# A decoder layer's second down projection in scaled float16 pairs, with sums of w_down and seven PSUM banks in turn

## The chip, the cores and the metric

The kernel runs on one core of a Trainium2 chip. The metric is the device time of one execution in microseconds (us), as a median over several runs. The core's engines are TensorE (PE in the profile; its weight loads are PEld), VectorE (DVE), ScalarE (ACT), GpSimd (POOL) and SyncE (SP, whose queue issues nearly all DMA transfers here). Each engine takes its instructions in the order in which the program gives them, and engines wait for each other through semaphores.

## The reference

The layer takes x of 2048 rows by 1024 columns and one condition vector. In order: a normalised and modulated x goes through one combined projection; eight heads of forgetting attention and a gated short convolution share its columns; their outputs go through `w_out` and are added to x. The second block is the one that matters here:

```python
h2 = rmsnorm(x, norm2_g) * (1 + sc2) + sh2
u = causal_dwconv(h2 @ w_up, ffn_conv_w)      # 1024 -> 2 x 2816, three taps over the rows
u_gate, u_val = jnp.split(u, 2, axis=-1)
y = (jax.nn.silu(u_gate) * u_val) @ w_down    # 2816 -> 1024, the down projection
return x + g2 * y
```

All inputs and the output are float32. `g2` is a row of 1024 gates that comes from the condition vector.

## The kernel before, in words

Every float32 product is made of three TensorE products of two parts, high and low: high x high, high x low, low x high (helper `mm3`, line 142). The parts are either float32r tiles or float16 tiles. Float16 parts need their operands scaled into float16's range, so stages that use them first find the largest magnitude of both operands, take powers of two from it, multiply by these when they split, and divide the result again. Float32r parts need no scale.

The feed-forward block goes in two halves of 1024 rows, `for hv in range(2)`: first the up projection `up(hv)`, then the down projection `down(hv, side)`.

`up(hv)` goes over 22 column blocks of 128 (`NPAIR = 22`). A block is seven products of 12 float16 matmuls (line 1253); VectorE and ScalarE combine them, apply three taps, silu and the gate product, and write y for the block to `y_sc` in DRAM. The last steps of a block, `finish`, run while TensorE is in the next block, and those of the last block run in the down projection that follows, as the first part of `side`. At the end of the 22 blocks `first_pairs(hv)` loads three pairs for the down projection and splits them.

`down(hv, side)` goes over four groups n (two blocks of 512 rows by two blocks of 512 output columns) of 22 steps i each. A step uses one pair: a `raw` tile whose first 512 columns are y of block i, transposed, and whose last 512 are the rows of `w_down` of block i. `load_pair` fills it (lines 1218 and 1219) and `split_pair` makes the float32r parts: ScalarE copies to `hi` (line 1224), VectorE subtracts to `lo` (line 1225). Four PSUM tiles `acc` of 128 rows by 512 columns take the products, 3 matmuls each, 12 per step. Steps 20 and 21 of a group run together, tile after tile, so that the four tiles end one after the other. Then `add_gated` (lines 1070 and 1071) multiplies each by the gates, adds x and stores the rows. `hi`, `lo` and `raw` have four buffers each. In the program a pair is split two steps before its use and loaded five steps before. `acc` comes from `ps_d`, which has four of the eight PSUM banks; `ps_u` has three more, which the up projection uses in its odd blocks, and `ps_n` one.

In the first half, `side` also has the second half's preparation, a piece at each even step: row norms of eight 128-row tiles (`norm2(2)` and `norm2(3)`: squares at line 1111, a root in small VectorE steps, a scaling at line 1118), then per column block four transposes on TensorE into the one bank of `ps_n` (line 1094), a read-out (line 1096) and float16 parts (lines 1077 and 1080). After these come the first weights of the second up projection.

The order of the work is the order of the code: nearly all instructions are pinned by `keep_in_program_order`, separately for each engine. A semaphore wait stands where a tile is read after a write, or written after a read, by another engine.

Of the kernel before, what the change touches and what calls it, by code (L numbers as in the profile page):

```python
# [20 lines left out]
P = 128  # L21
S = 2048
D = 1024
# [7 lines left out]
NPAIR = DFF // P  # L31
# [8 lines left out]
HS = 1.0  # L40
LINES = 528
NTEMP = 7


@with_exitstack
def kernel(
# [20 lines left out]
    V, A, G, T = nc.vector, nc.scalar, nc.gpsimd, nc.tensor  # L67
    x, c, out = x[0], c[0:1], out[0]
# [69 lines left out]
    K = tc.keep_in_program_order  # L138
# [597 lines left out]
    def load_out(n):  # L736
# [9 lines left out]
            lambda: K(A.activation(wo["junk"][:, 0:512], t, AF.Abs, accum_out=sums[:, n : n + 1])),  # L746
        )

    def out_scales(pool):
# [8 lines left out]
        K(V.tensor_reduce(gm[:, 0:1], pt[0:2, 0:P], axis=AX.X, op=ALU.max))  # L758
        K(V.tensor_scalar(gm, ident[0:2, 0:2], gm[:, 0:1], None, op0=ALU.mult))
# [3 lines left out]
        bits = osc.bitcast(I32)  # L763
        K(V.tensor_scalar(osc, pt[:, 0:2], 2.0**-40, 2.0**60, op0=ALU.max, op1=ALU.min))
        K(V.tensor_scalar(bits, bits, 0x7F800000, None, op0=ALU.bitwise_and))
        K(V.reciprocal(osc, osc))
        K(V.tensor_scalar(bits, bits, 0x7F800000, None, op0=ALU.bitwise_and))
        K(V.tensor_scalar(osc, osc, 16384.0, None, op0=ALU.mult))
        K(V.tensor_tensor(oinv, osc[:, 0:1], osc[:, 1:2], op=ALU.mult))
        K(V.reciprocal(oinv, oinv))  # L770
        yield

    def load_mixed(Q, i):
# [282 lines left out]
    with ExitStack() as ph:  # L1056
# [7 lines left out]
        def wide_temp():  # L1064
            return fp.tile([P, 1040], F32, tag="w4", name="w4", bufs=5)[:, 0:1026]

        def add_gated(acc, gate, src, dst):

            g = temp()
            K(V.tensor_tensor(g, acc, gate, op=ALU.mult))  # L1070
            K(V.tensor_tensor(src, src, g, op=ALU.add))
            nc.sync.dma_start(dst, src)

        bt = {}

        def high(raw, hi):
            K(A.activation(hi, raw, AF.Copy))  # L1077
# [21 lines left out]
        def norm2(Q):  # L1099

            if Q == 0:
                fp.tile([P, 96], F32, name="rim2")
            ss = fp.tile([P, 16], F32, tag="ss", name="ss", bufs=2)[:, 0:4]
            xn[Q] = kept[Q] if Q < 2 else [wide_temp()[:, 0:D] for _ in range(4)]
            if Q >= 2:
                for t in range(4):
                    K(nc.sync.dma_start(xn[Q][t], x1_sc[Q * 4 + t]))
                yield
            for t in range(4):
                junk = fp.tile([P, D], BF16, tag="t2", name="junk", bufs=NTEMP)  # L1110
                K(A.activation(junk, xn[Q][t], AF.Square, accum_out=ss[:, t : t + 1]))
                if t % 2:
                    yield
            K(V.tensor_scalar(ss, ss, 1.0 / D, EPS, op0=ALU.mult, op1=ALU.add))
            for ins in rsqrt_steps(fp, ss, 4, "r"):
                K(ins)
            for t in range(4):
                K(V.tensor_scalar(xn[Q][t], xn[Q][t], ss[:, t : t + 1], None, op0=ALU.mult))
# [36 lines left out]
            if Q % 2:  # L1155
                low(t4, *t4s)
                yield
# [56 lines left out]
        def load_pair(n, i):  # L1214

            Q, hf = divmod(n, 2)
            raw = raw_tile()
            K(nc.sync.dma_start(raw[:, 0:512], y_sc[i][:, Q * 512 : (Q + 1) * 512]))
            K(nc.sync.dma_start(raw[:, 512:1024], w_down[i * P : (i + 1) * P, hf * 512 : (hf + 1) * 512]))
            return raw  # L1220

        def split_pair(raw):
            hi, lo = pair_tiles()
            K(A.activation(hi, raw, AF.Copy))  # L1224
            K(V.tensor_tensor(lo, raw, hi.bitcast(F32), op=ALU.subtract))  # L1225
            y, wd = halves((hi, lo))
            return (*y, *wd)

        raws, pairs = {}, {}

        def first_pairs(hv):

            for i in range(3):
                raws[4 * hv, i] = load_pair(4 * hv, i)
            yield
            for i in range(3):
                pairs[4 * hv, i] = split_pair(raws.pop((4 * hv, i)))
                yield
            while True:
                yield  # L1240

        def up(hv):
# [25 lines left out]
            def finish(i, p1, Y, gate, val, yg):  # L1268

                taps(yg, gate, i)  # L1270
                add(val[:, 2:514], p1, Y)
                yield
                yv = tap(val, NPAIR + i)
                keep_halo(val, NPAIR + i)
                K(A.activation(yg, yg, AF.Silu))
                taps(yv, val, NPAIR + i)
                yield
                K(V.tensor_tensor(yv, yg, yv, op=ALU.mult))
                nc.sync.dma_start(y_sc[i][:, hv * 1024 : (hv + 1) * 1024], yv)
                yield  # L1280

            wts, ops = ready.pop("wts"), ready.pop("ops")
            last = None
            for i in range(NPAIR):
                o11, o12, os2, os4, os3, o22, os1 = ops
                X, Y, Z = [
# [37 lines left out]
                yg = tap(gate, i)  # L1324
                keep_halo(gate, i)
                next(wts)
                product(Y, o22, "t4", False)
                last = finish(i, p1, Y, gate, val, yg)
            return last

        def down(hv, side):

            todo = [(n, i) for n in range(4 * hv, 4 * hv + 4) for i in range(NPAIR)]
            loaded = split = 3
            for e, (n, i) in enumerate(todo):
                Q, n0 = n // 2, n % 2 * 512
                rows = [slice((Q * 4 + t) * P, (Q * 4 + t + 1) * P) for t in range(4)]
                while split < min(e + 3, len(todo)):
                    if loaded == split:
                        raws[todo[loaded]] = load_pair(*todo[loaded])  # L1340
                        loaded += 1
                    pairs[todo[split]] = split_pair(raws.pop(todo[split]))
                    split += 1
                while loaded < min(e + 6, len(todo)):
                    raws[todo[loaded]] = load_pair(*todo[loaded])
                    loaded += 1
                if i == 0:
                    acc = [ps_d.tile([P, 512], F32, tag="d", name="acc") for _ in range(4)]
                if i == NPAIR - 3:
                    xs = [fb.tile([P, 512], F32, tag=f"src{n % 2 * 4 + t}", name="xs") for t in range(4)]  # L1350
                    for xp, r in zip(xs, rows):
# [8 lines left out]
                    next(side, None)  # L1360
                if i == NPAIR - 1:
                    for t in range(4):
                        add_gated(acc[t], gates[:, D + n0 : D + n0 + 512], xs[t], out[rows[t], n0 : n0 + 512])
            for _ in side:
                pass

# [39 lines left out]
```

## Time and profile before

| what | us |
|---|---|
| median of 3 runs (lowest, highest) | 2449.33 (2448.84, 2451.18) |
| the profiled execution's own time | 2450.66 |
| its span from first to last instruction | 2448.8 |
| TensorE busy | 2366.2 |
| first half's down projection, start to end | 1554 to 1806 |
| second half's up projection | 1806 to 2204 |
| second half's down projection | 2204 to the end |

The stage borders come from the chain of waits, where TensorE's groups of matmuls change their line (1253 in the up projection, 142 in the down projection). Matmuls are pipelined and their ends are modelled, so the length of one is not what it costs; in a run without breaks its cost is the time from one start to the next. In a row of a timeline the columns are start, length, engine, line, operation, output and inputs, count, and in brackets the idle time before it with what ended it. In a row of the groups the two numbers behind the bar are the busy time of all and the mean of one in ns. A wait is given to the semaphore that came last.

### The profile page before, as it was taken

The numbers are of one execution on the slowest core, as the hardware profiler recorded it, in microseconds if no ns is written. First come the engines' busy times: TensorE is split into PE (matmuls) and PEld (weight loads), VectorE is DVE, ScalarE is ACT, GpSimd is POOL, SyncE is SP. The second block draws the span as 40 slices with busy tenths as digits, with TensorE's granted clock in tenths as the row PEclk, the third lists the DMA queues.
The fourth block names the chain that finished last, engine by engine and source line by source line (L and its number), as shares of the span: only waits on it lengthen the run. The fifth ranks groups of instructions, "written<-read, shape, count | busy, mean of one in ns | idle before, by whom it ended". The sixth has DMA issues, their size and how long they took to land.

```text
span 2448.8 us, 38397 instructions
## 1 busy us (share of the span) xinstructions
PE 2366.2 (97%) x14451; PEld 1590.2 (65%) x14451; DVE 1773.1 (72%) x3329; ACT 1262.6 (52%) x2024; POOL 336.4 (14%) x282
## 2 busy tenths in 40 slices
PE   5999999999898888999999999999999999999999
PEld 5988788888676666444444444688864444448887
DVE  6567884542798888556888888757768888885554
ACT  5433453220688887343666565555545556554333
POOL 0210101101567785001000000000000000000000
PEclk9999999999999999999999999999999999999999
DMA  9344686543699988534222222677742222236775
GB/s 278 116 131 125 179 239 184 159 134 90 123 187 166 213 166 159 184 104 155 78 86 86 87 88 76 202 241 225 226 146 81 91 86 86 87 100 215 228 228 184
DMA packets 428706, 368.70 MB, mean 151 GB/s; under 512 B 184208, under 2 KB 327912, under 8 KB 427496
## 3 DMA queue, kind: packets, MB, share of 16 engines
q1 hardware_dynamic: 421400, 349.40, 51.1%
q10 hardware_dynamic: 4752, 8.46, 1.0%
q0 software_dynamic: 2368, 8.39, 0.9%
q8 instruction: 113, 1.85, 0.3%
q14 instruction: 73, 0.60, 0.1%
HBM read 267.54 MB, written 65.08 MB: 136 GB/s over the span
## 4 chain that ended last, share of the span: by engine, by line
PE 79%; DVE 7%; issue 5%; DMA 4%; ACT 3%; POOL 1%; SPq 0%; ACTq 0%; DVEq 0%; POOLq 0%
PE acc L1253 33%; PE acc L142 25%; PE pr L142 11%; PE pv L142 3%; DMA far<-wide 2%; PE pt L937 1%; PE ps L876 1%; DMA wx<-in_w_up_dram 1%; PE ps L877 1%; DVE near L944 1%; DVE s_t L900 1%; PE po L973 1%; ACT s_t L917 1%; PE po L975 1%; PE po L974 1%
## 5 line engine op out<-in xcount | busy, mean ns | idle before, releaser
L1253 PEld LDWEIGHTS <-pair 128*128 128x128 f16 x3696 | 361.4, 98 | 436.2 <-issue 0.3
L1253 PE MATMUL acc<-t,pair 128*128 128x512 f16 x2112 | 477.4, 379 | 0.0
L1253 PE MATMUL acc<-b,pair 128*128 128x512 f16 x1584 | 363.5, 379 | 0.0
L1225 DVE TENSOR_TENSOR lo<-raw,hi 128x1024 fp32r<-128x1024 f32 x176 | 211.9, 1223 | 153.6 <-ACT hi L1224 153.3
L142 PE MATMUL acc<-hi 128*128 128x512 f32 x704 | 276.8, 393 | 1.6 <-DVE t L1070 1.6
L142 PE MATMUL acc<-lo,hi 128*128 128x512 f32 x704 | 274.3, 390 | 0.5 <-DVE lo L1225 0.5
L142 PE MATMUL acc<-hi,lo 128*128 128x512 f32 x704 | 274.3, 390 | 0.0
L1224 ACT ACTIVATE hi<-raw 128x1024 fp32r<-128x1024 f32 x176 | 182.4, 1055 | 178.2 <-PE acc L142 141.2
L1266 DVE SCALAR_TENSOR_TENSOR w<-w,fcw,w 128x1024 f32<-128x1024 f32 x176 | 226.1, 1285 | 34.7 <-ACT w L1261 25.4
L1077 ACT ACTIVATE pair<-raw 128x1024 f16<-128x1024 f32 x132 | 138.3, 1048 | 68.4 <-DVE raw L1160 68.3
L142 PE MATMUL acc<-wp,mp 128*128 128x512 f16 x768 | 171.1, 382 | 1.0 <-DVE raw L829 1.0
L1261 ACT ACTIVATE w<-w,fcw 128x1024 f32<-128x1024 f32 x88 | 100.7, 1144 | 130.7 <-DVE w L1159 130.7
L917 ACT ACTIVATE s_t<-s_t,nb,cst 128x2048 f32<-128x2048 f32 (+15 forms) x128 | 164.7, 1288 | 4.8
L1080 DVE TENSOR_TENSOR pair<-raw,pair 128x1024 f16<-128x1024 f32 x132 | 160.7, 1218 | 4.7 <-ACT pair L1077 4.7
L608 ACT ACTIVATE wx<-wx 128x512 f32<-128x512 f32 x88 | 55.6, 632 | 198.8 <-DMA wx<-in_w_up_dram 171.1
L142 PE MATMUL pr<-hh,wh 128*128 128x512 f32 x384 | 153.4, 399 | 0.0
L142 PEld LDWEIGHTS acc<-hi 128*128 128x128 f32 x704 | 132.2, 188 | 31.2 <-DVE t L1070 4.4
L142 PE MATMUL pr<-hl,wh 128*128 128x512 f32 x384 | 151.1, 393 | 0.0
L142 PE MATMUL pr<-hh,wl 128*128 128x512 f32 x384 | 150.8, 393 | 0.2 <-DVE wl L179 0.2
L142 PEld LDWEIGHTS acc<-lo,hi 128*128 128x128 f32 x704 | 132.3, 188 | 27.8 <-DVE lo L1225 1.0
L142 PEld LDWEIGHTS acc<-hi,lo 128*128 128x128 f32 x704 | 132.2, 188 | 27.7
L929 POOL TENSOR_TENSOR wide<-s_t,wide 128x1024 f16<-128x1024 f32 x64 | 136.9, 2138 | 5.3
(296 smaller groups left out, 4694.4 us busy)
## 6 DMA issues: line engine op xcount, KB each, us to landing
raw<-in_w_up_dram SPq DMA_DIRECT2D x88, 512.0 KB, 3.9
raw<-y_sc SPq DMA_DIRECT2D x176, 256.0 KB, 4.3
raw<-in_w_down_dram SPq DMA_DIRECT2D x176, 256.0 KB, 6.1
wx<-in_w_up_dram SPq DMA_DIRECT2D x88, 256.0 KB, 3.1
y_sc<-w SPq DMA_DIRECT2D x44, 512.0 KB, 2.6
wm<-in_w_ada_dram SPq DMA_DIRECT2D x128, 128.0 KB, 2.8
wr<-in_w_in_dram SPq DMA_DIRECT2D x40, 256.0 KB, 3.9
x_t<-in_x_dram SPq DMA_DIRECT2D x16, 512.0 KB, 5.5
```

Source lines behind the costliest of these rows:

```text
L142: ins = T.matmul(acc, lhsT=a, rhs=b, start=st, stop=sp)
L608: K(A.activation(t, t, AF.Abs, accum_out=l1[:, n : n + 1]))
L876: K(T.matmul(ps[:, 0:cw], lhsT=qt, rhs=kh[:, c0 : c0 + cw], start=True, stop=False))
L917: K(A.activation(cols, cols, AF.Exp, bias=nb[:, p : p + 1], scale=qk[:, 4:5], accum_out=un["l"][:, p : p + 1]))
L929: K(G.tensor_tensor(wide[:, 1, :], s_t[:, WB * P : WU], wide[:, 0, :], op=ALU.subtract))
L1077: K(A.activation(hi, raw, AF.Copy))
L1080: K(V.tensor_tensor(lo, raw, hi, op=ALU.subtract))
L1224: K(A.activation(hi, raw, AF.Copy))
L1225: K(V.tensor_tensor(lo, raw, hi.bitcast(F32), op=ALU.subtract))
L1253: K(T.matmul(acc, lhsT=a, rhs=b, start=st, stop=sp, skip_group_check=True))
L1261: K(A.activation(y, u[:, 0:1024], AF.Copy, scale=fcw[:, ct : ct + 1]))
L1266: K(V.scalar_tensor_tensor(y, u[:, m : m + 1024], fcw[:, m * 44 + ct : m * 44 + ct + 1], y, op0=ALU.mult, op1=ALU.add))
```

## The change

In the second half, `split_pair` makes float16 pairs for the first 20 of the 22 blocks (`LAST = 20`): one instruction per engine for y and one for `w_down`, each with its power of two. Blocks 20 and 21 keep float32r parts, scaled alike. `add_gated` multiplies by the inverse scale too. The scales come from sums of absolute values, per partition, an upper bound for the largest magnitude. For `w_down` they are taken in the first half's groups n = 0 and 1: after each split, ScalarE writes the absolute values of the pair's `w_down` half over itself and keeps the sum. For y they are taken in the second up projection, one ScalarE instruction of 128x1024 per block for blocks 0 to 19. In its last block, `first_pairs(1)` reduces both, with two small TensorE products, and the vector helper `powers_of_two` (moved out of `out_scales` unchanged) makes the scales. In both halves `first_pairs` now splits two pairs, later in the last block, and the third is split at the start of `down`. The PSUM tiles of the groups take the banks of `ps_d` and `ps_u` in turn, seven in all.

The core of the diff:

```diff
-        def split_pair(raw):
-            hi, lo = pair_tiles()
-            K(A.activation(hi, raw, AF.Copy))
-            K(V.tensor_tensor(lo, raw, hi.bitcast(F32), op=ALU.subtract))
-            y, wd = halves((hi, lo))
-            return (*y, *wd)
+        def split_pair(n, e, i, raw):
+
+            if n < 4:
+                hi, lo = pair_tiles()
+                K(A.activation(hi, raw, AF.Copy))
+                K(V.tensor_tensor(lo, raw, hi.bitcast(F32), op=ALU.subtract))
+                if n < 2:
+                    K(A.activation(raw[:, 512:1024], raw[:, 512:1024], AF.Abs, accum_out=big["rim"][:, 52 + n * NPAIR + i : 53 + n * NPAIR + i]))
+                y, wd = halves((hi, lo))
+                return (*y, *wd)
+            scales = big["rim"][:, 46:48]
+            if i < LAST:
+                t = fq.tile([P, 2048], F16, tag=("hi", "lo")[e % 2], name="yw", bufs=4)
+                parts = [[t[:, (2 * n + m) * 512 : (2 * n + m + 1) * 512] for m in range(2)] for n in range(2)]
+            else:
+                parts = halves(pair_tiles())
+            for n, (hi, lo) in enumerate(parts):
+                half, sc = raw[:, n * 512 : (n + 1) * 512], scales[:, n : n + 1]
+                K(A.activation(hi, half, AF.Copy, scale=sc))
+                K(V.scalar_tensor_tensor(lo, half, sc, hi if i < LAST else hi.bitcast(F32), op0=ALU.mult, op1=ALU.subtract))
+            return (*parts[0], *parts[1])
...
         def first_pairs(hv):
 
+            rim = big["rim"]
+            om, sc, inv, gm = rim[:, 44:46], rim[:, 46:48], rim[:, 48:49], rim[0:2, 50:52]
             for i in range(3):
                 raws[4 * hv, i] = load_pair(4 * hv, i)
-            yield
-            for i in range(3):
-                pairs[4 * hv, i] = split_pair(raws.pop((4 * hv, i)))
+            if hv:
+                K(V.tensor_reduce(om[:, 0:1], rim[:, 0:LAST], axis=AX.X, op=ALU.max))
+                K(V.tensor_reduce(om[:, 1:2], rim[:, 52 : 52 + 2 * NPAIR], axis=AX.X, op=ALU.max))
+            yield
+            if hv:
+                pt = ps_n.tile([P, 512], F32, tag="n", name="pt")
+                K(T.transpose(pt[0:2, 0:P], om, ident))
+                K(V.tensor_reduce(gm[:, 0:1], pt[0:2, 0:P], axis=AX.X, op=ALU.max))
+                K(V.tensor_scalar(gm, ident[0:2, 0:2], gm[:, 0:1], None, op0=ALU.mult))
+            yield
+            if hv:
+                pt = ps_n.tile([P, 512], F32, tag="n", name="pt")
+                K(T.matmul(pt[:, 0:2], lhsT=ones[0:2, :], rhs=gm, start=True, stop=True))
+                powers_of_two(pt[:, 0:2], sc, inv)
+            yield
+            yield
+            for i in range(2):
+                pairs[4 * hv, i] = split_pair(4 * hv, i, i, raws.pop((4 * hv, i)))
                 yield
...
+                if hv and i < LAST:
+                    junk = fp.tile([P, D], BF16, tag="t2", name="junk", bufs=NTEMP)
+                    mags.append(lambda: K(A.activation(junk, yv, AF.Abs, accum_out=big["rim"][:, i : i + 1])))
                 nc.sync.dma_start(y_sc[i][:, hv * 1024 : (hv + 1) * 1024], yv)
...
-            loaded = split = 3
+            loaded, split = 3, 2
...
-                    acc = [ps_d.tile([P, 512], F32, tag="d", name="acc") for _ in range(4)]
+                    acc = []
+                    for c in range(4 * (n - 4 * hv), 4 * (n - 4 * hv) + 4):
+                        acc.append((ps_d if c % 7 < 4 else ps_u).tile([P, 512], F32, tag="d" if c % 7 < 4 else "u", name="acc"))
```

The gating becomes `scalar_tensor_tensor(g, acc, inv, gate, mult, mult)` in the second half.

What moves on ScalarE's queue, in the first half's down projection, group n = 0, around the first column of the second half's preparation. `hi` is a pair's high half, `t2` the read-out of four transposes, `b11` and `b21` its float16 high part. Before:

```order
L1224 ACTIVATE hi_18297<-raw_18242 128x1024 [waits DMAHW0_49,DMAHW7_49,DVE_49,PE_49]
L1096 ACTIVATE t2_18321<-pt_18316,sh2_137,a2_136 128x512 [waits PE_49]
L1077 ACTIVATE b11_18323<-t2_18321 128x512 [waits Activation_49]
L1224 ACTIVATE hi_18326<-raw_18261 128x1024 [waits DMAHW2_49,DMAHW1_49,DVE_49]
L1224 ACTIVATE hi_18345<-raw_18282 128x1024 [waits DMAHW4_49,DMAHW3_49,DVE_49]
L1096 ACTIVATE t2_18369<-pt_18364,sh2_137,a2_136 128x512 [waits PE_49]
```

With the change, at the same place (L1237 is the absolute sum of `w_down`, L1234 the high half, L1104 the read-out, L1085 the high part):

```order
L1234 ACTIVATE hi_18313<-raw_18256 128x1024 [waits DMAHW7_49,DMAHW0_49,PE_49]
L1237 ACTIVATE raw_18256,rim2_13816<-raw_18256 128x512 [waits DVE_49]
L1104 ACTIVATE t2_18338<-pt_18333,sh2_137,a2_136 128x512 [waits PE_49]
L1085 ACTIVATE b11_18340<-t2_18338 128x512 [waits Activation_49]
L1234 ACTIVATE hi_18343<-raw_18276 128x1024 [waits DMAHW2_49,DMAHW1_49]
L1237 ACTIVATE raw_18276,rim2_13816<-raw_18276 128x512 [waits DVE_49]
L1234 ACTIVATE hi_18363<-raw_18298 128x1024 [waits DMAHW4_49,DMAHW3_49]
L1237 ACTIVATE raw_18298,rim2_13816<-raw_18298 128x512 [waits DVE_49]
L1104 ACTIVATE t2_18388<-pt_18383,sh2_137,a2_136 128x512 [waits PE_49]
```

Behind each high half stands a sum that waits for VectorE and writes the `raw` tile that the low half reads.

On TensorE's queue, in the last block of the second up projection, between its second product (operand `t2`) and its third (operand `b21`). Before:

```order
L1253 LDWEIGHTS pair_22914
L1253 MATMUL acc_23030<-t2_19634,pair_22914 128x512
L1253 LDWEIGHTS pair_22915
L1253 MATMUL acc_23030<-t2_19634,pair_22915 128x512
L1253 LDWEIGHTS pair_22912
L1253 MATMUL acc_23029<-b21_18371,pair_22912 128x512 [waits Activation_49]
```

With the change:

```order
L1293 LDWEIGHTS pair_22996
L1293 MATMUL acc_23114<-t2_19678,pair_22996 128x512
L1293 LDWEIGHTS pair_22997
L1293 MATMUL acc_23114<-t2_19678,pair_22997 128x512
L1266 MATMUL pt_23169<-ident_117,rim2_13816 2x128 [waits DVE_49,PE_49]
L1293 LDWEIGHTS pair_22994
L1293 MATMUL acc_23113<-b21_18390,pair_22994 128x512 [waits Activation_49]
```

The small transposition of the two maxima stands between the products and waits for VectorE. The second small product, of the same kind, stands one product later.

More of the change, by code (lines that the diff above doesn't have):

```diff
@@ L42 @@
 NTEMP = 7
+LAST = 20
 @with_exitstack
@@ L747, in load_out, with powers_of_two @@
         )
+    def powers_of_two(src, s, inv):
+        bits = s.bitcast(I32)
+        K(V.tensor_scalar(s, src, 2.0**-40, 2.0**60, op0=ALU.max, op1=ALU.min))
+        K(V.tensor_scalar(bits, bits, 0x7F800000, None, op0=ALU.bitwise_and))
+        K(V.reciprocal(s, s))
+        K(V.tensor_scalar(bits, bits, 0x7F800000, None, op0=ALU.bitwise_and))
+        K(V.tensor_scalar(s, s, 16384.0, None, op0=ALU.mult))
+        K(V.tensor_tensor(inv, s[:, 0:1], s[:, 1:2], op=ALU.mult))
+        K(V.reciprocal(inv, inv))
     def out_scales(pool):
@@ L1065, in wide_temp, with add_gated @@
             return fp.tile([P, 1040], F32, tag="w4", name="w4", bufs=5)[:, 0:1026]
-        def add_gated(acc, gate, src, dst):
+        def add_gated(hv, acc, gate, src, dst):
             g = temp()
-            K(V.tensor_tensor(g, acc, gate, op=ALU.mult))
+            if hv:
+                K(V.scalar_tensor_tensor(g, acc, big["rim"][:, 48:49], gate, op0=ALU.mult, op1=ALU.mult))
+            else:
+                K(V.tensor_tensor(g, acc, gate, op=ALU.mult))
             K(V.tensor_tensor(src, src, g, op=ALU.add))
             nc.sync.dma_start(dst, src)
-        bt = {}
+        bt, big = {}, {}
         def high(raw, hi):
@@ L1101, in norm2 @@
             if Q == 0:
-                fp.tile([P, 96], F32, name="rim2")
+                big["rim"] = fp.tile([P, 96], F32, name="rim2")
             ss = fp.tile([P, 16], F32, tag="ss", name="ss", bufs=2)[:, 0:4]
@@ L1283, in up @@
             last = None
+            mags = []
             for i in range(NPAIR):
@@ L1341, in down @@
                         loaded += 1
-                    pairs[todo[split]] = split_pair(raws.pop(todo[split]))
+                    pairs[todo[split]] = split_pair(todo[split][0], split, todo[split][1], raws.pop(todo[split]))
                     split += 1
@@ L1362, in down @@
                     for t in range(4):
-                        add_gated(acc[t], gates[:, D + n0 : D + n0 + 512], xs[t], out[rows[t], n0 : n0 + 512])
+                        add_gated(hv, acc[t], gates[:, D + n0 : D + n0 + 512], xs[t], out[rows[t], n0 : n0 + 512])
             for _ in side:
```

13 lines of the change are left out of this document (5 added, 8 removed).

## The prediction

> **What bounds the kernel now.** I read the page first, then the chain of waits from 1400 us on, then the busy times by stage. Times in all fences are microseconds from the span's start unless marked ns. From the page:
>
> ```profile
> span 2448.8 us, 38397 instructions
> PE 2366.2 (97%) x14451; PEld 1590.2 (65%) x14451; DVE 1773.1 (72%) x3329; ACT 1262.6 (52%) x2024; POOL 336.4 (14%) x282
> ```
>
> TensorE carries the program, so two things can move the time: how far apart matmuls start, and moments in which TensorE waits for split operands. The chain of waits shows the first (start, length, what):
>
> ```profile
> 1805.90 398.88 PE acc L1253 x1848
> 2204.78 235.32 PE acc L142 x1038
> ```
>
> The up projection (float16) starts a matmul every 398.88 / 1848 = 215.8 ns, the second half's down projection (float32r) every 235.32 / 1038 = 226.7 ns. Both run without a break. The busy times by stretch show the first column group of the first half's down projection, then the second up projection:
>
> ```profile
> core 0: us, PE busy (x) PEld busy (x) DVE busy (x) ACT busy (x) POOL busy (x), PEclk, DMA share, GB/s
> 1554.40:1619.00 64.60, 64.20 (x290) 52.43 (x288) 42.71 (x55) 33.44 (x41) 0.00 (x0) 1.00 0.72 236
> 1806.00:2204.40 398.40, 398.40 (x1848) 180.52 (x1847) 347.73 (x389) 227.84 (x302) 0.00 (x0) 1.00 0.28 88
> ```
>
> TensorE is all but full at the whole clock, ScalarE is half idle. By these shares 0.6 us more ScalarE work per pair would be free. But a pair is made in a chain over two engines, and the change lengthens that chain.
>
> **The change part by part.** *The sums of w_down (the main term).* In the first half's groups n = 0 and 1, each of 44 splits gets a third step: ScalarE writes the high half, VectorE subtracts the low half, and then ScalarE takes absolute values in place over the half of `raw` that VectorE has just read. So this step waits for the low half (the order shows a wait on VectorE at L1237), and ScalarE's next instruction, the next pair's high half, stands behind it. High, low and sum of one pair follow the sum of the pair before: a loop. Its lengths, from timelines of ScalarE and VectorE and from the groups:
>
> ```profile
> 2300.04 1.06 ACT L1224 ACTIVATE hi<-raw 128x1024 fp32r<-128x1024 f32 x1 [1.66 <-PE acc L142]
> 2301.13 1.23 DVE L1225 TENSOR_TENSOR lo<-raw,hi 128x1024 fp32r<-128x1024 f32 x1 [1.49 <-ACT hi L1224]
> ...
> L746 ACT ACTIVATE junk<-wo 128x512 bf16<-128x512 f32 x16 | 9.9, 622 | 0.0
> ...
> 1729.48 0.61 DVE t L1087
> ...
> 1730.12 0.77 ACT t L1077 x2
> ```
>
> High to low 1.09 us (2300.04 to 2301.13), low half 1.23, VectorE to ScalarE 0.03 (the chain piece at 1730), the sum 0.62 as in L746, the nearest row, also absolute values of 128x512 with a sum: 2.97 us. TensorE uses up a pair in 12 x 226.7 = 2.72 us. From here ScalarE sets the pace, and whatever else it or VectorE does in between adds in full:
>
> ```profile
> 1553.80 1.04 ACT L1224 ACTIVATE hi<-raw 128x1024 fp32r<-128x1024 f32 x1
> 1557.08 1.16 ACT L1261 ACTIVATE w<-w,fcw 128x1024 f32<-128x1024 f32 x1 [2.23 <-DVE w L1159]
> ...
> 1601.67 0.78 ACT L1096 ACTIVATE t<-pt,sh,a 128x512 f32<-128x512 f32 x1 [2.59 <-PE pt L1094]
> ...
> 1603.02 2.00 ACT L1224 ACTIVATE hi<-raw 128x1024 fp32r<-128x1024 f32 x2
> ...
> 1654.00 1.04 ACT L1111 ACTIVATE junk<-w 128x1024 bf16<-128x1024 f32 x1
> ...
> 1655.04 1.04 ACT L1111 ACTIVATE junk<-w 128x1024 bf16<-128x1024 f32 x1
> ...
> 1584.03 0.16 DVE L1114 TENSOR_SCALAR ss<-ss 128x4 f32<-128x4 f32 x1
> 1586.40 1.42 DVE L1118 TENSOR_SCALAR w<-w,ss 128x1024 f32<-128x1024 f32 x2
> ...
> 1558.26 2.60 DVE L1266 SCALAR_TENSOR_TENSOR w<-w,fcw,w 128x1024 f32<-128x1024 f32 x2
> 1614.41 0.68 DVE L1070 TENSOR_TENSOR t<-acc,gates 128x512 f32<-128x512 f32 x1
> 1619.71 1.22 DVE L1225 TENSOR_TENSOR lo<-raw,hi 128x1024 fp32r<-128x1024 f32 x1
> ```
>
> - 8 normalised columns, each a read-out and a high half between two splits, 1601.67 to 1603.02 = 1.35: 10.8. One more read-out alone: 0.7.
> - 8 squares of 1.04 (1654.00 to 1655.04): 8.3.
> - 2 row-norm scalings on VectorE, 1584.03 to 1587.82 = 3.8. VectorE idles 2.97 - 1.23 = 1.74 per loop, so 2.05 of each shows: 4.1.
> - Gating group n = 0, 1614.41 to 1619.71 = 5.3 on VectorE, less the same 1.74: 3.5.
> - The last up column's rest (tap 1.16 and silu of the same size on ScalarE; on VectorE four taps, 1.3 each): 2.6 where ScalarE has to wait for both, 1.3 where only VectorE is late: 3.9.
>
> Sum of these: 31.3 us. Pair 1's high half starts at about 1553.8, as the first one behind the tap does today. Pair 43's then starts at 1553.8 + 42 x 2.97 + 31.3 = 1709.8; its low half is done 2.3 later, at 1712.1, and 24 matmuls (5.4) end group 1 at 1717.5. Today:
>
> ```profile
> 1680.67 0.48 PE L142 MATMUL acc<-hi 128*128 128x512 f32 x1
> 1681.98 0.50 PE L142 MATMUL acc<-hi 128*128 128x512 f32 x1 [0.36 <-DVE t L1070]
> ```
>
> Group 2 begins at 1680.67, so TensorE is 37 us late. From there no sums are taken, and I add 1 for the refill of the pairs behind the next gating: **+38**. Bounds: with a loop of 2.72 instead of 2.97, +27; with 0.1 more per pair for hand-overs, and raw buffers late by as much again, +45. I take the row values.
>
> *Seven banks.* Today TensorE waits for gating at the three group ends of the first half: the fence above shows two matmuls of one tile's start 1.31 apart instead of 0.68. All such waits together are small:
>
> ```profile
> PE acc L142 <- DVE t L1070: 1.6, 5, 0.4
> ```
>
> In starts lost that is about 3 us. With three free banks they go, but at the first two ends pairs are late anyway, which the 38 already has; at most 0.8 at the third end is kept, and it lies inside that rounding. Second half: no waits, nothing to gain.
>
> *Float16 in the second half.* 4 groups x 20 pairs x 12 = 960 matmuls change type: 960 x (226.7 - 215.8) = **-10.4**. A switch from float16 to float32r costs once:
>
> ```profile
> 2204.43 0.58 PE L142 MATMUL acc<-hi 128*128 128x512 f32 x1
> 2204.84 0.39 PE L142 MATMUL acc<-lo,hi 128*128 128x512 f32 x1
> 2205.07 0.39 PE L142 MATMUL acc<-hi,lo 128*128 128x512 f32 x1
> ```
>
> 0.41 instead of 0.23. The last two pairs of each group stay float32r: three switches more, **+0.6**. The splits become two instructions on each engine:
>
> ```profile
> L781 ACT ACTIVATE mp<-src,rim 128x512 f16<-128x512 f32 x32 | 22.1, 712 | 11.7 <-DVE wp L782 11.7
> L782 DVE SCALAR_TENSOR_TENSOR mp<-src,rim,mp 128x512 f16<-128x512 f32 x32 | 23.4, 749 | 11.9 <-ACT mp L781 11.8
> ```
>
> 1.42 and 1.50 per pair in a step of 12 x 215.8 = 2.59: hidden by TensorE. Not so at the start: only two pairs are split ahead instead of three, and VectorE has four low halves (6.0) and five column instructions (5.9) from about 2205 on before pair 4, wanted 4 x 2.59 = 10.4 after TensorE's start at 2204.4. That is late by 1.7 (0 to 3): **+1.7**.
>
> The Trainium skill, page "TensorE: Matmul & The Clock Gate", section "Back-to-back issue gap", gives a warm matmul N/2.4 + 2.5 ns, 215.8 at 512 columns, whatever its type. The float16 rows agree, the float32r rows lie 10.9 above. By the rule alone the type would bring nothing.
>
> *The scale.* Two tiny matmuls enter TensorE's queue in the last up column, the second behind VectorE's maximum and scaling; today VectorE does that pair of operations, for w_out, in
>
> ```profile
> L759 DVE TENSOR_SCALAR rim<-ident,rim 2x2 f32<-2x2 f32 x1 | 0.7, 731 | 0.0
> L758 DVE TENSOR_REDUCE rim<-pt 2x1 f32<-2x128 f32 x1 | 0.3, 280 | 0.1
> ```
>
> Here they follow an addition that today begins at 2193.46 and takes 0.68, so they end near 2195.1. TensorE arrives at 2194.25, after the third product of the column:
>
> ```profile
> 2193.46 0.68 DVE L1159 TENSOR_TENSOR t<-t,acc 128x512 f32<-128x512 f32 x1
> 2194.25 5.34 PE L1253 MATMUL acc<-t,pair 128*128 128x512 f16 x24
> ```
>
> 0.8 of waiting, two type switches and two small matmuls: **+1.5** (0.5 to 3).
>
> *The rest.* 20 sums over y in the second up projection, some 1.04 each: ScalarE is busy 227.84 of 398.4 there and 21 more fit; the next queued read-out waits for TensorE anyway. 0, or up to 21 if that cover went. The final gating multiplies twice, 746 ns (L829 is this form on a PSUM tile) for 685, four times behind the last matmul: **+0.2**.
>
> ```profile
> L829 DVE SCALAR_TENSOR_TENSOR raw<-acc,rim,raw 128x512 f32<-128x512 f32 x16 | 11.6, 746 | 13.3 <-PE acc L142 13.2
> L1070 DVE TENSOR_TENSOR t<-acc,gates 128x512 f32<-128x512 f32 x32 | 21.9, 685 | 9.0 <-PE acc L142 9.0
> ```
>
> Sum: 38 - 10.4 + 0.6 + 1.7 + 1.5 + 0.2 = +31.6 on the profiled execution's 2450.7 (its span 2448.8 and 1.9 around it): 2482.3. It lies 1.3 above the median of the runs, so 2481.0.
>
> **The rivals.** *The sums are free* (faster). If ScalarE's sum found the low half done, because VectorE kept far enough ahead, or the next high half did not queue behind it, 38 would become -0.8 or so: 2481 - 39 = 2442. It decides as soon as the loop, with all that stands in it, is under TensorE's pace, 2.72. For it: the half-idle ScalarE, and buffers for four pairs. Against it: two high halves run back to back (1603.02, x2) right after the read-out of a column, so waiting instructions do hold those behind them; and 2.97 is over 2.72 before anything else is added.
>
> *A shorter loop* (slower, less). With 2.72 per loop the +27 gives 2470; should half of the listed extras also overlap, 16 less, about 2455.
>
> *Loads join the loop* (slower still). A `raw` buffer is now free after the sum instead of after the low half. From the page's DMA issues:
>
> ```profile
> raw<-in_w_down_dram SPq DMA_DIRECT2D x176, 256.0 KB, 6.1
> ```
>
> Landing takes 6.1 us. With four buffers a load has three loops, 8.9, for issue and landing. At 10.3 for both, each loop is (10.3 + 2.97) / 4 = 3.3: 42 x 0.35 = 15 more, 2496. TensorE's slower pace thins the traffic, which speaks against it.
>
> *Float16 brings nothing.* Without the -10.4: 2491. Against it stand w_out's products, float16 pairs through the same helper, 382 ns a matmul where float32r has 390:
>
> ```profile
> L142 PE MATMUL acc<-wp,mp 128*128 128x512 f16 x768 | 171.1, 382 | 1.0 <-DVE raw L829 1.0
> L142 PE MATMUL acc<-hi,lo 128*128 128x512 f32 x704 | 274.3, 390 | 0.0
> ```
>
>
> **How the numbers follow.** What this kernel's measurement can tell from no change is about 0.2%, 5 us. Forecast 72%, 2481, its own range 2468 to 2488 from the bounds +27 and +45. Shorter loop 9%, of which 2 within 0.2% of today; loads 7%; no gain from float16 4%; free sums 8%, of which 1 ends within 0.2%. Faster 7%, same 3%, slower 90%. The range for 8 in 10 is 2465 to 2490: it leaves out the free sums, the shortest loop and most of the loads.
>
> **What would show it.** In the changed kernel's first down projection, groups 0 and 1 should last about 82 us each instead of 64, TensorE idle before `acc` until the low half, ScalarE's sums idle 1.2 to 1.3 us each before them until `lo`, and the sum group x44 at about 0.62. Groups 2 and 3 should keep 61 to 64. The second down projection should start matmuls 216 ns apart, 227 in the last 24 of each group, with a break of 1 to 2 us near pair 4. If ScalarE's sums show no wait for `lo`, the main term is wrong; if the up projection gets breaks, the y sums are not hidden.

## The result and the profile after

The change makes the kernel slower. The median is 2478.1 us (2474.09 to 2479.35, 4 runs) against 2450.26 us (2448.84 to 2454.34, 4 runs) for the kernel before. The ratio is 1.0113, with a 95% interval of 1.0098 to 1.0128. The profiled execution took 2478.72 us, with a span of 2477.0. Forecast were 2481 us and a range of 2465 to 2490.

The head of the page of the kernel after:

```profile
span 2477.0 us, 38721 instructions
PE 2371.2 (96%) x14454; PEld 1506.9 (61%) x14454; DVE 1793.0 (72%) x3428; ACT 1333.3 (54%) x2240; POOL 336.3 (14%) x282
```

The shares hardly move (ScalarE from 52% to 54%, TensorE from 97% to 96%), and from them alone nobody would find 28 us. The stages do show it. The table gives the time from a stage's first matmul to the next stage's first one, from TensorE's timeline; the last column is the time from the last matmul's start to the end of the span.

| kernel | start of the 1st up projection | 1st up | 1st down | 2nd up | 2nd down | tail |
|---|---|---|---|---|---|---|
| before | 1155.40 | 398.67 | 251.67 | 398.68 | 239.35 | 5.06 |
| after | 1154.51 | 398.67 | 289.33 | 399.58 | 229.71 | 5.21 |
| difference | -0.89 | 0 | +37.66 | +0.90 | -9.64 | +0.15 |

The part ahead of the first up projection holds nothing of the change and differs between executions: it starts there between 1149.9 and 1155.8 in the eleven profiles of this case. What follows repeats to some hundredths of a microsecond wherever two kernels have the same code. So the experiments below are read by these stages, and by the medians for the whole.

The first down projection loses 37.66 us, and the second gains 9.64. The busy times by stretch of the kernel after show its first three column groups and the second up projection:

```profile
core 0: us, PE busy (x) PEld busy (x) DVE busy (x) ACT busy (x) POOL busy (x), PEclk, DMA share, GB/s
1553.20:1635.60 82.40, 71.63 (x282) 53.14 (x281) 42.12 (x51) 48.92 (x86) 0.00 (x0) 0.94 0.62 190
1635.60:1714.90 79.30, 71.21 (x289) 53.17 (x288) 39.66 (x53) 47.65 (x84) 0.00 (x0) 0.96 0.60 191
1714.90:1782.00 67.10, 64.73 (x286) 52.45 (x285) 52.83 (x65) 32.92 (x42) 0.00 (x0) 0.97 0.65 209
1842.50:2242.10 399.60, 399.49 (x1853) 181.13 (x1853) 347.28 (x399) 244.98 (x341) 0.00 (x0) 1.00 0.27 86
```

In the same columns, groups n = 0 and 1 of the kernel before:

```profile
1554.07:1615.87 61.80, 61.80 (x281) 51.12 (x280) 39.98 (x51) 32.93 (x41) 0.00 (x0) 1.00 0.72 235
1615.87:1679.77 63.90, 63.38 (x290) 51.76 (x288) 39.99 (x54) 33.80 (x42) 0.00 (x0) 1.00 0.76 251
```

Groups n = 0 and 1, where sums of `w_down` are taken, last 82.4 and 79.3 us; before, they lasted 61.8 and 63.9. ScalarE is idle for 33.5 of the 82.4, so it isn't short of time. What it waits for stands in its timeline:

```profile
1571.57 1.04 ACT L1234 ACTIVATE hi<-raw 128x1024 fp32r<-128x1024 f32 x1
1573.90 0.63 ACT L1237 ACTIVATE raw<-raw 128x512 f32<-128x512 f32 x1 [1.29 <-DVE lo L1235]
1574.44 0.19 ACT L1237 ACTIVATION_READ_ACCUMULATOR raw<-raw 128x1 f32 x1
1574.53 1.05 ACT L1234 ACTIVATE hi<-raw 128x1024 fp32r<-128x1024 f32 x1
```

and in VectorE's, in the same microseconds:

```profile
1572.64 1.22 DVE L1235 TENSOR_TENSOR lo<-raw,hi 128x1024 fp32r<-128x1024 f32 x1 [1.74 <-ACT hi L1234]
```

From 1571.57 to 1574.53 one turn takes 2.96 us: high half on ScalarE, low half on VectorE, sum on ScalarE, next high half. ScalarE idles 1.29 per turn for VectorE, VectorE 1.74 for ScalarE, and TensorE wants a pair every 2.72. In the waits ScalarE's row for this has one entry for each of the 44 sums (first fence, ScalarE, first half's down projection), and nearly all of TensorE's own waits are for the two parts of a pair (second fence, from there to the end):

```profile
ACT raw L1237 <- DVE lo L1235: 68.3, 44, 4.8
...
ACT hi L1234 <- DMA raw<-y_sc: 3.0, 1, 3.0
...
ACT hi L1234 <- DMA raw<-in_w_down_dram: 1.0, 1, 1.0
```

```profile
PE acc L143 <- DVE lo L1235: 15.2, 18, 1.9
PE acc L143 <- ACT hi L1234: 4.4, 6, 1.0
```

### The profile page after: what moved, and what is told of

Same layout as the page of the kernel before. It is cut to its first block, busy times and chain, and to the rows that moved or that the text cites. A ratio compares the mean times of both kernels' runs of the same rounds, so it can differ in the third digit from the quotient of the medians.

```text
span 2477.0 us, 38721 instructions
## 1 busy us (share of the span) xinstructions
PE 2371.2 (96%) x14454; PEld 1506.9 (61%) x14454; DVE 1793.0 (72%) x3428; ACT 1333.3 (54%) x2240; POOL 336.3 (14%) x282
## 4 chain that ended last, share of the span: by engine, by line
PE 73%; DVE 9%; issue 6%; DMA 6%; ACT 5%; POOL 2%; SPq 0%; ACTq 0%; DVEq 0%; POOLq 0%
PE acc L1293 32%; PE acc L143 20%; PE pr L143 11%; PE pv L143 3%; DVE lo L1235 2%; DMA wx<-in_w_up_dram 2%; DMA far<-wide 2%; PE pt L942 1%; ACT hi L1234 1%; DVE near L949 1%; PE ps L881 1%; DVE s_t L905 1%; PE ps L882 1%; PE po L978 1%; DMA raw<-in_w_down_dram 1%
## 5 line engine op out<-in xcount | busy, mean ns | idle before, releaser
L143 PE MATMUL acc<-yw 128*128 128x512 f16 x960 | 208.0, 379 | 0.6 <-DVE yw L1249 0.6
L1085 ACT ACTIVATE pair<-raw 128x1024 f16<-128x1024 f32 x132 | 138.3, 1048 | 81.7 <-DVE raw L1168 81.7
L143 PE MATMUL acc<-lo,hi 128*128 128x512 f32 x384 | 157.5, 410 | 15.2 <-DVE lo L1235 15.2
L1235 DVE TENSOR_TENSOR lo<-raw,hi 128x1024 fp32r<-128x1024 f32 x88 | 106.3, 1222 | 82.5 <-ACT hi L1234 74.3
L143 PEld LDWEIGHTS <-yw 128*128 128x128 f16 x960 | 93.7, 98 | 114.2 <-issue 1.7
L143 PE MATMUL acc<-hi 128*128 128x512 f32 x384 | 156.4, 407 | 4.4 <-ACT hi L1234 4.4
L143 PE MATMUL acc<-hi,lo 128*128 128x512 f32 x384 | 153.6, 400 | 0.0
L1248 ACT ACTIVATE yw<-raw,rim 128x512 f16<-128x512 f32 x160 | 105.8, 714 | 78.2 <-DMA raw<-y_sc 40.1
L1249 DVE SCALAR_TENSOR_TENSOR yw<-raw,rim,yw 128x512 f16<-128x512 f32 x160 | 111.0, 747 | 38.3 <-ACT yw L1248 38.1
```

What stands on the lines that cost most here:

```text
L143: ins = T.matmul(acc, lhsT=a, rhs=b, start=st, stop=sp)
L1248: K(A.activation(hi, half, AF.Copy, scale=sc))
L1249: K(V.scalar_tensor_tensor(lo, half, sc, hi if i < LAST else hi.bitcast(F32), op0=ALU.mult, op1=ALU.subtract))
```

## The experiments

Theory A, the prediction's: the sum is written in place, so it has to wait until VectorE has read `raw`, and the next pair's high half queues behind it. Two engines with time to spare then take turns and are slower than TensorE. Theory B: the sums and the other new work load ScalarE too much. In B, the place that a sum is written to makes no difference. Results are medians, each set against runs of the kernel before that were taken beside it.

**Sums written elsewhere.** In the kernel after, the sums' output goes to a free tile, so that ScalarE needn't wait for VectorE:

```diff
-    K(A.activation(raw[:, 512:1024], raw[:, 512:1024], AF.Abs, accum_out=...))
+    K(A.activation(big["sink"][:, 0:512], raw[:, 512:1024], AF.Abs, accum_out=...))
```

> The changed kernel, but the absolute values of w_down are written to a tile of their own (a weight tile that is free at that time) and no longer over the raw tile; the sums are the same. ScalarE's sum then has nothing to wait for. Theory A (high half, low half and sum form one serial loop of 2.97 us): the loop is gone, first down projection back from 289 to about 252 us, time 2478 - 37 = 2441 (2438 to 2445). Theory B (the 44 x 0.63 = 28 us of added ScalarE work are what costs, whatever it waits for): the work stays, time 2468 or more.

Measured: 2444.51 us (10 runs) against 2450.58, ratio 0.9979 (0.9968 to 0.999). The first down projection lasts 255.75 us instead of 289.33. ScalarE does the same work, with the sum right behind its high half and no idle time between:

```profile
1579.22 1.04 ACT L1234 ACTIVATE hi<-raw 128x1024 fp32r<-128x1024 f32 x1
1580.17 0.62 ACT L1237 ACTIVATE sink<-raw 128x512 bf16<-128x512 f32 x1
```

So 33.6 of the 37.66 us hang on where an output nobody reads is put. The stage stays some 4 us above the 252 that Theory A gave; where they come from is found below, with the third pair.

**Each sum taken twice.** As above, with a second sum of the same operands (at a line of its own, 1238):

```diff
+    K(A.activation(big["sink"][:, 512:1024], raw[:, 512:1024], AF.Abs, accum_out=...))
     K(A.activation(big["sink"][:, 0:512], raw[:, 512:1024], AF.Abs, accum_out=...))
```

> As the run with the sums written elsewhere, but each sum is taken twice: 28 us more ScalarE work in the same 44 places, with no wait for VectorE. Theory A: ScalarE has 1.05 + 1.26 = 2.3 us of work per pair of 2.72, so plain pairs stay hidden and only the places with columns and squares show, about 6 us over that run: 2447 (2442 to 2452). Theory B: 28 us over that run.

Measured: 2448.79 us (10 runs), ratio 0.9997 (0.9987 to 1.0008). The timeline of ScalarE shows the pair of sums:

```profile
1575.14 0.61 ACT L1237 ACTIVATE sink<-raw 128x512 bf16<-128x512 f32 x1
...
1575.88 0.63 ACT L1238 ACTIVATE sink<-raw 128x512 bf16<-128x512 f32 x1
```

The first down projection grows from 255.75 to 261.40. That is 5.65 us for 44 more sums, at least 27.7 us of work. Twice the sums without the wait cost less than once with it. Theory B falls.

**The sums short.** In place again, over 64 columns instead of 512: the wait stays, the sum itself shrinks.

```diff
-    K(A.activation(raw[:, 512:1024], raw[:, 512:1024], AF.Abs, accum_out=...))
+    K(A.activation(raw[:, 512:576], raw[:, 512:576], AF.Abs, accum_out=...))
```

> The changed kernel, but the sums of w_down, still in place and waiting for the low half, go over 64 of the 512 columns only (the scale then rests on a part of w_down). Theory A: the sum falls from 0.63 to about 0.25, the loop from 2.97 to 2.58, 42 x 0.39 = 16 less: 2462 (2457 to 2467), and the idle time before each sum stays at 1.29. Theory B: 44 x 0.39 = 17 less, the same. A part of the loss that comes from neither (loads, the later split of the first pairs) would leave it above 2467.

Measured: 2464.77 us (4 runs), ratio 1.0058 (1.0039 to 1.0078). From ScalarE's timeline:

```profile
1570.38 0.26 ACT L1237 ACTIVATE raw<-raw 128x64 f32<-128x64 f32 x1 [1.29 <-DVE lo L1235]
...
1570.64 1.05 ACT L1234 ACTIVATE hi<-raw 128x1024 fp32r<-128x1024 f32 x1
...
1573.23 1.04 ACT L1234 ACTIVATE hi<-raw 128x1024 fp32r<-128x1024 f32 x1
```

The time doesn't tell A from B here, as both expected the same; the timeline does. The turn is 2.59 us, shorter by the 0.37 that the sum lost, and the wait is still 1.29. A turn of 2.59 is below TensorE's 2.72, and yet the first down projection stays 23.94 us longer than before (275.61 against 251.67): the column read-outs, squares, row norms and gating stand in the same line of turns, as the list in the prediction has them.

**The sums alone.** The kernel before with the sums in place and nothing else of the change:

```diff
     K(V.tensor_tensor(lo, raw, hi.bitcast(F32), op=ALU.subtract))
+    if n < 2:
+        K(A.activation(raw[:, 512:1024], raw[:, 512:1024], AF.Abs, accum_out=...))
```

> The kernel before with one part of the change alone: the sums of w_down in place in groups 0 and 1 of the first down projection; nothing uses them. Theory A: all of the loss and none of the gain, 2450 + 38 = 2488 (2484 to 2492). If the seven banks or the two instead of three pairs split ahead have a share in the loss, it comes out lower, 2480 or less.

Measured: 2486.55 us (4 runs), ratio 1.0153 (1.0131 to 1.0174). From the first up projection on it takes 38.56 us more than the kernel before: 33.33 in the first down projection and 5.23 already in the last block of the up projection, where three pairs are split ahead and their sums hold up a read-out of ScalarE:

```profile
PE acc L1255 <- ACT t L1318: 3.4, 1, 3.4
```

The sums alone thus account for the loss. The rest of the change, from +38.56 to +29.07 for the whole, is a gain of 9.5.

**The seven banks, alone and left out.** First the kernel before with the banks in turn, then the kernel with sums elsewhere and four banks:

```diff
-    acc = [ps_d.tile([P, 512], F32, tag="d", name="acc") for _ in range(4)]
+    acc = []
+    for c in range(4 * (n - 4 * hv), 4 * (n - 4 * hv) + 4):
+        acc.append((ps_d if c % 7 < 4 else ps_u).tile([P, 512], F32, tag="d" if c % 7 < 4 else "u", name="acc"))
```

> The kernel before with the seven PSUM banks alone. TensorE's waits for gating (1.6 us idle, some 3 us in starts) at the three group ends of the first down projection should go; what the late pairs then cost instead is open. First down projection 251.7 -> 249 to 251, time 1 to 3 us under before. Nothing in the second.

> The changed kernel with the sums written elsewhere, and with four banks as before. If the seven banks earn something once the loop is gone, the first down projection grows from 255.8 by 1 to 3 us and so does the time (2444.5 -> 2447); if pairs are what is late at the group ends, it stays within 0.5 us.

Measured: the banks alone 2445.56 us (10 runs) against 2448.92, ratio 0.9991 (0.998 to 1.0002); the first down projection is 1.95 us shorter than before. Without them, with sums elsewhere: 2446.15 us (10 runs), ratio 0.9988 (0.9979 to 0.9997), and the stage is 1.82 us longer than with them. TensorE's waits for gating are gone in the one, where only waits for pairs are left, and there in the other; the first row is of the banks alone:

```profile
PE acc L142 <- DVE lo L1225: 1.3, 2, 0.8
```

and the row of the kernel with sums elsewhere and four banks:

```profile
PE acc L143 <- DVE t L1078: 2.5, 8, 0.4
```

By the stages the banks are worth 1.8 to 2.0 us when pairs come in time. That is too little for the medians: the first ratio's interval includes 1.

**Three pairs split ahead in the first half.** The change also splits only two pairs ahead. With sums elsewhere, the first half gets its third one back (the second half has to wait for its scale and keeps two):

```diff
+            if hv == 0:
+                for i in range(3):
+                    pairs[0, i] = split_pair(0, i, i, raws.pop((0, i)))
+                    yield
+                while True:
+                    yield
...
-            loaded, split = 3, 2
+            loaded, split = 3, 2 if hv else 3
```

> The changed kernel with the sums written elsewhere, and in the first half three pairs split early in the last up block, as before the change (two only in the second half, where the scale comes late). If the 4 us that the first down projection still has over the kernel before (255.8 against 251.7) come from the missing third pair, it falls to about 252 and the time to 2440 or 2441, below both kernels; if they come from ScalarE's added work, it stays at 255.

Measured: 2440.07 us (2436.26 to 2444.63, 6 runs) against 2448.92, ratio 0.9963 (0.9951 to 0.9975). It beats both kernels. The first down projection takes 250.64 us, 5.11 less than with two pairs and 1.03 less than before. All that TensorE still waits for, from there to the end:

```profile
PE acc L143 <- DVE lo L1235: 1.3, 2, 0.8
PE acc L143 <- DVE yw L1249: 0.6, 1, 0.6
PE acc L143 <- ACT hi L1234: 0.4, 1, 0.4
```

The same in the kernel after, with the sums in place:

> The changed kernel, sums in place, with three pairs split early in the first half. If the missing third pair has a share of 4 us in the loss, first down projection 289.3 -> 285 and time 2474; if the loop sets the pace from the first pair on, whatever the lead, the lead is used up and nothing changes: 2478.

Measured: 2476.44 us (4 runs), ratio 1.0112 (1.0099 to 1.0125); from the first up projection on it takes 1322.62 us, where the kernel after takes 1322.50. Nothing is gained in all: the down projection is 5.07 shorter, but the up projection is 5.22 longer, which the expectation hadn't foreseen, with the read-out held up as in the sums alone:

```profile
PE acc L143 <- DVE lo L1235: 13.6, 16, 1.9
PE acc L1299 <- ACT t L1366: 3.4, 1, 3.4
```

Where ScalarE and VectorE take turns from the first pair on, an earlier start only moves the stall. Without the turns the same edit is worth 5.1 us.

**Each sum one split later.** In place, but queued behind the next pair's high half (with three pairs ahead):

```diff
     K(V.tensor_tensor(lo, raw, hi.bitcast(F32), op=ALU.subtract))
+    while sums_due:
+        sums_due.pop(0)()
     if n < 2:
-        K(A.activation(raw[:, 512:1024], ..., AF.Abs, accum_out=...))
+        sums_due.append(lambda: K(A.activation(raw[:, 512:1024], ..., AF.Abs, accum_out=...)))
```

> The changed kernel with three pairs split early in the first half and the sums in place, but each sum is queued on ScalarE one split later, behind the next pair's high half. The write over the raw tile and its wait for the low half stay. Theory A: the low half runs while ScalarE makes the next high half, so the wait is over when the sum is reached, and ScalarE has 1.05 + 0.63 us per pair of 2.72: first down projection about 251, time 2440 as with the sums written elsewhere. What could keep it above 2445: the raw buffer comes free one high half later, with two loops instead of three for the next load (landing 4 to 6 us), so loads could now be late.

Measured: 2442.57 us (8 runs) against 2448.58, ratio 0.9973 (0.9963 to 0.9984). The first down projection takes 252.99 us. Two rows of ScalarE's waits, from 1545 to 1680 us:

```profile
ACT hi L1234 <- DMA raw<-in_w_down_dram: 10.2, 8, 3.4
...
ACT raw L1239 <- DVE lo L1235: 5.3, 6, 1.9
```

The write in place and the work are the same as in the kernel after; only the place in ScalarE's queue differs. So what costs is not the write as such, but that a waiting instruction stands ahead of the high half for which VectorE idles. The 2.35 us that this stage takes more than in the version with sums elsewhere and three pairs weren't followed to their end. A `raw` tile is free later here, but the waits for loads don't show that to be the cause: in all of this stage ScalarE's high halves wait 10.2 us for loads of `w_down` here, 6.7 in that version and 12.1 in the kernel before.

## Why the prediction was right, and where not

- **Main term**, +38, measured +37.66. The steps also hold one by one. The turn was put at 2.97 and is 2.96. Pair 1's high half starts at 1552.86 in ScalarE's timeline and pair 43's at 1708.06: 155.2 us, forecast 156.0. Less 42 turns of 2.96, the work between them comes to 30.9, listed as 31.3. By ScalarE's timeline, what the turns take beyond 2.96 is 10.6 for the eight columns (listed as 10.8), 0.7 for the read-out alone (0.7), 8.3 for the squares (8.3), 3.8 for the scalings (4.1), 3.5 for the gating (3.5) and 3.9 for the last up column (3.9). The gating's 3.5 is the wait of 4.77 below, less the usual 1.29:

```profile
1642.06 0.63 ACT L1237 ACTIVATE raw<-raw 128x512 f32<-128x512 f32 x1 [4.77 <-DVE lo L1235]
...
1708.06 1.04 ACT L1234 ACTIVATE hi<-raw 128x1024 fp32r<-128x1024 f32 x1
1710.40 0.63 ACT L1237 ACTIVATE raw<-raw 128x512 f32<-128x512 f32 x1 [1.29 <-DVE lo L1235]
```

- **Its last part** has small errors that cancel by luck. Groups 0 and 1 together are 36.0 us longer than before (161.7 against 125.7), not 37. The refill in group 2, put at 1, costs 2.6 (67.1 against 64.5); 1.4 of that is a slow clock, which the last section shows and the forecast had no term for. Group 3 takes 0.9 less. The bounds are a little off their own terms: 0.1 more per pair, twice, over 42 turns is 8.4, so +46 and not +45, and +27 leads to 2470, not to the 2468 of the forecast's own range.
- **Two pairs ahead** were priced only for the second half. For the first half, I began with "pair 1's high half starts at about 1553.8, as the first one behind the tap does today", which holds (1552.86, in a stage that itself starts 0.9 earlier), and so the missing third pair had no term. It needs none in the kernel after, where the turns set the end whatever was split ahead. But it is worth 5.1 us as soon as they are gone. The rival in which the sums are free was therefore too low. It had 7.3 us under the median before (2442 against 2449.3); freed of their wait, the sums leave 4.5 from the first up projection on (1288.90 against 1293.43).
- **Seven banks**: at most 0.8, inside the main term. Alone they give 1.95 and, with sums elsewhere, 1.82. What they bring within the kernel after wasn't separated from the late pairs.
- **Float16**, -10.4 + 0.6 + 1.7 = -8.1, measured -9.64. 960 matmuls at 215.8 are right. The step that failed is the **type switch**, "0.41 instead of 0.23", three times. In TensorE's timeline of the kernel after, at a switch in the second down projection:

```profile
2294.05 0.81 PE L143 MATMUL acc<-yw 128*128 128x512 f16 x3
2294.51 0.58 PE L143 MATMUL acc<-hi 128*128 128x512 f32 x1
2294.93 0.40 PE L143 MATMUL acc<-lo,hi 128*128 128x512 f32 x1
```

  The last float16 matmul of the first row starts two gaps of 0.216 behind 2294.05, near 2294.48. The first float32r one follows 0.03 later, the next 0.42 after that. Together that is 0.45 for two starts, and 0.216 + 0.227 = 0.443 is what they cost anyway. I had read the long gap and not the short one ahead of it. A switch costs nothing that shows here. The rival in which float16 brings nothing fell with this stage's 9.64.
- **The start of the second down projection**, +1.7 (0 to 3), was a single break of half that size, near pair 4. The row before it in TensorE's timeline has 37 starts:

```profile
2244.68 8.15 PE L143 MATMUL acc<-yw 128*128 128x512 f16 x37
2253.48 2.75 PE L143 MATMUL acc<-yw 128*128 128x512 f16 x12 [0.65 <-DVE yw L1249]
```

  The 37th start is at 2244.68 + 36 x 0.2158 = 2252.45. To 2253.48 it is 1.03, 0.8 more than a usual gap. VectorE's work ahead of that pair was listed as 6.0 + 5.9 = 11.9 us from 0.6 behind TensorE's start on, which by itself gives 2.1 rather than 1.7; in its timeline it takes 11.0, from 2242.41 to 2253.43, and begins 0.3 behind. With no cost for switches the sum is -10.4 + 0.8 = -9.6, as measured, to within the 0.2 by which the stage border moves (next point).
- **The scale**, +1.5, measured +0.7 of the second up projection's +0.90. TensorE and VectorE there:

```profile
2228.44 0.27 PE L1266 MATMUL pt<-ident,rim 128*2 128x128 f32 x1
2228.55 2.75 PE L1293 MATMUL acc<-b,pair 128*128 128x512 f16 x12
2231.41 0.38 PE L1272 MATMUL pt<-rim,ones 2*128 2x2 f32 x2
2231.72 1.47 PE L1293 MATMUL acc<-t,pair 128*128 128x512 f16 x6
```

```profile
2230.84 0.27 DVE L1267 TENSOR_REDUCE rim<-pt 2x1 f32<-2x128 f32 x1
2231.14 0.22 DVE L1268 TENSOR_SCALAR rim<-ident,rim 2x2 f32<-2x2 f32 x1
```

  The scaling of 2x2 takes 0.22, not the 0.73 of the row I took it from (L759 of the kernel before, one record). TensorE's wait, put at 0.8, shrinks by as much: 12 x 0.216 from 2228.55 on end at 2231.14, and the second small product follows at 2231.41, 0.27 later. Around the first product TensorE loses 0.1 (2228.44 to 2228.55), around the second 0.6: the row of 12 has its last start at 2228.55 + 11 x 0.2158 = 2230.92, and the next row begins 0.80 later instead of 0.22. The other 0.2 is the stage border. Before, the first float32r matmul of the down projection followed the last float16 one by 0.03, as at a switch; now it is float16 and follows by 0.22, and the long gap of 0.41 behind the short one, which counted in the next stage, is gone.
- **Sums of y**, 0: the second up projection keeps TensorE busy for 399.49 of 399.60 us with ScalarE at 244.98, and its +0.9 is the scale's 0.7 and the border's 0.2. **Tail**, +0.2: measured +0.15.
- **Of the rivals**, loads didn't join the turns: ScalarE's high halves wait 4.0 us for loads in all of the first down projection of the kernel after, in two waits, both behind the last turn. The 10.3 us for issue and landing in that rival came from no row; landing took 3.2 to 6.8 there. The shorter loop fell with the turn of 2.96.

The sum of the stages, +37.66 + 0.90 - 9.64 + 0.15 = +29.1, stands against +31.6 forecast. Of the 2.5 between them, taken by stages, 1.5 is the float16 term and 0.6 the scale.

## What to carry to other kernels

A small piece of work on a half-idle engine is free only if its place in that engine's queue is: ask for which engine it waits, and which instruction behind it that engine is itself waiting for. If the answer closes a circle, the circle's length counts against the pace of the bound engine, with everything else that stands in it, whatever the shares of busy time say. Write an output that nobody reads where nobody else reads, or queue the instruction one step later; the first turned this change from a loss of 28 us into a gain of 6, the second, with the third pair split ahead again, into one of 6 as well.

## What the hardware showed beyond that

TensorE's clock came down for a few microseconds at a time where it was starved. One such place in the first down projection of the kernel after, from TensorE's timeline:

```profile
1590.26 0.39 PE L143 MATMUL acc<-hi,lo 128*128 128x512 f32 x1
1591.64 0.49 PE L143 MATMUL acc<-hi 128*128 128x512 f32 x1 [0.99 <-ACT hi L1234]
1592.90 0.50 PE L143 MATMUL acc<-lo,hi 128*128 128x512 f32 x1 [0.76 <-DVE lo L1235]
...
1593.60 0.63 PE L143 MATMUL acc<-hi 128*128 128x512 f32 x1
1594.03 0.63 PE L143 MATMUL acc<-lo,hi 128*128 128x512 f32 x1
1594.45 0.63 PE L143 MATMUL acc<-hi,lo 128*128 128x512 f32 x1
```

and the busy times of the stretch that follows, where the granted clock is the number behind the busy times:

```profile
1593.20:1596.60 3.40, 3.40 (x10) 2.60 (x9) 1.92 (x7) 2.11 (x6) 0.00 (x0) 0.51 0.43 116
```

After 2.64 us with only one start in between, matmuls start 0.427 apart instead of 0.227 and the granted clock is 0.51, here for 3 us. There are five such stretches in that stage, with 39 slow gaps: 39 x 0.2 = 7.8 us of TensorE's time. This is why its first two groups show a mean clock of 0.94 and 0.96, where the kernel before has 1.00. With three pairs split ahead and the sums in place there are five as well, and the sums alone have three. The kernel with short sums has none, though pairs come late there too, with single gaps of up to 2.09 us, and neither have the versions with sums elsewhere or one split later. The Trainium skill, page "TensorE: Matmul & The Clock Gate", section "Why this matters for your kernels", asks for no idle gap over some 3 us. In the kernel after the clock fell after gaps that were each shorter, the longest of them 2.28. What decides it isn't shown: the same two gaps, 1.38 and 1.26, at 1582.26 were followed by no slow stretch, and neither were 1.38 and 1.79 at 1564.83.

Little of the 7.8 us reaches the end. From 1552.8 to 1708.1, ScalarE waits for nothing but low halves (63.3 us in 42 waits), so the first four stretches only used time that TensorE would have idled. The fifth, in group 2, counts. There the chain of waits comes back to TensorE:

```profile
1722.89 10.02 PE acc L143 x35
```

At 0.227 a start, 35 matmuls would take 7.9. Seven of the 39 slow gaps lie here, 1.4 us, and the one wait that TensorE still has behind them in the group, 0.5 us for a low half, was there before the change too. No run took the clock's part away by itself.
